# Seven products for eight in two gate and up blocks of each feed-forward stage

## The chip, the cores and the metric

The kernel runs on one core of a Trainium2 chip. The metric is the device time of one execution in microseconds, the median of three runs. A TensorE matmul here takes a 128x128 left operand and 512 columns of the right one, in float32r.

## The reference, cut to what matters

Two blocks over 256 tokens of width 1024 follow each other. Each is: feed-forward, mixer, feed-forward. The four feed-forward stages have this form, with `D_FF` = 2816:

```
def swiglu(x, w_gate, w_up, w_down):
    return (jax.nn.silu(x @ w_gate) * (x @ w_up)) @ w_down
x = x + 0.5 * swiglu(rms_norm(x, ffn1_norm[l]), ffn1_w_gate[l], ffn1_w_up[l], ffn1_w_down[l])
```

The first mixer is an attention with an indexer that picks 64 keys a query, beside a pool over windows; the second is a gated mixer with a short convolution. A final norm closes the program.

## The kernel before

Every product is done in three matmuls (`mm3`, L68): both operands are split into a high part that fits float32r and the rest, and hi*hi, hi*lo and lo*hi are summed in PSUM. Weights come in chunks of 128 x 2048 (1 MB). `weights` (L54) loads one from SP into a `raw` buffer (3 of them); `split` (L64) has ScalarE copy it into `whi` and VectorE subtract to `wlo` (4 pairs). The activations lie transposed and split in `hT`, written once a stage.

`rows` (L95) multiplies four k tiles of one chunk with both token tiles: 2 x 4 x 3 = 24 matmuls. In `ffn` (L219) blocks j = 0 to 4 hold 512 columns of gate and 512 of up, two chunks each for the two halves of the contraction; block 5 holds the last 256 of both in two chunks. `gated` (L226) applies Silu on ScalarE and the product on VectorE, both from PSUM; `turned` (L106) transposes the result on TensorE and splits it into `act`. Then the down projection runs in two halves f of six chunks. Work put in `late` (the transposes) is traced behind a later chunk by `flush` (L88). All PSUM tiles come from one rotation of eight banks, `ps` (L51).

Stage 1 starts with `cold_start` (L185), in pieces as the inputs land. The row norm is applied behind the matmuls: `rstd` (L133) takes a power on GpSimd (L86), and GpSimd does little else. The tables of the mixers are loaded from SP in the stage before (`meanwhile`, L260), the gain of the final norm in the last stage. At the end `y` (L722) is a `raw` buffer for each of the two token tiles; the four stores are issued at L736.

The program is written in a framework that takes the text as priority, works out the order on each engine and queue ahead of time by readiness, and sets the semaphores.

Of the kernel before, what the change touches and what calls it, by code (L numbers as in the profile page):

```python
# [10 lines left out]
F32 = mybir.dt.float32  # L11
# [6 lines left out]
P = 128  # L18
T = 256
# [15 lines left out]


class Block:
    def __init__(self, ctx, tc, a, out):
        self.tc, self.nc, self.a, self.out = tc, tc.nc, a, out
        pool = lambda name, bufs, **k: ctx.enter_context(tc.tile_pool(name=name, bufs=bufs, **k))  # L40
        self.const = pool("const", 1)
        self.raw = pool("raw", 3)
        self.wsp = pool("wsp", 4)
        self.big = pool("big", 1)
        self.work = pool("work", 2)
        self.small = pool("small", 4)
        self.psum = pool("psum", 8, space=PSUM)
        self.late = []


    def ps(self, shape=(P, 512)):  # L51
        return self.psum.tile(list(shape), F32, tag="ps", name="ps")

    def weights(self, src):  # L54

        n = src.shape[1]
        raw = self.raw.tile([P, 2048], F32, tag="raw", name="raw")[:, :n]
# [30 lines left out]
    def flush(self):  # L88

        late, self.late = self.late, []  # L90
        for f in late:
            f()
# [12 lines left out]

    def turned(self, dst, x, k):  # L106

        for t in range(2):
            n = x[t].shape[1] // P
            pt = self.ps((P, 4, P))  # L110
# [41 lines left out]
    def add(self, accs, f, scale, following, tiles=(0, 1)):  # L152
# [15 lines left out]
        def pair(k):  # L168
            pt = self.ps((P, 2, T))
# [6 lines left out]
        self.late += [lambda: pair(4 * f), lambda: pair(4 * f + 2)]  # L176


    def warm_up(self):

        ps = self.ps()
# [3 lines left out]
    def cold_start(self, accs, src):  # L185
# [33 lines left out]
    def ffn(self, n, following, first=False, meanwhile=None):  # L219
        nc, a = self.nc, self.a  # L220
        gu, d, d_end = a[f"gu{n}"], a[f"d{n}"], a[f"de{n}"]
        with self.tc.tile_pool(name="act", bufs=1) as pool:
            act = pool.tile([P, KF, 2, T], F32R, tag="act", name="act")
            r = None

            def gated(j, gs, us):  # L226
                prs = []
                for t in range(2):
                    w = gs[t].shape[1]
                    sg = self.work.tile([P, 512], F32, tag="sg", name="sg")[:, :w]  # L230
                    nc.scalar.activation(sg, gs[t], AF.Silu, scale=r[:, t : t + 1])  # L231
                    pr = self.work.tile([P, 512], F32, tag="pr", name="pr", bufs=4)[:, :w]
                    nc.vector.scalar_tensor_tensor(pr, us[t], r[:, t : t + 1], sg, op0=ALU.mult, op1=ALU.mult)  # L233
                    prs.append(pr)
                self.late.append(lambda: self.turned(act, prs, 4 * j))

            for j in range(6):
                G = [self.ps() for _ in range(2)]
                U = [self.ps() for _ in range(2)] if j < 5 else None
                if j == 0 and first:  # L240
                    self.cold_start((G, U), gu)
                    r = self.rstd()
                    gated(j, G, U)
                    continue
                self.token_major(G, gu[2 * j], 512, 0)
                self.flush()
                if j == 0:
                    self.token_major(U, gu[1], 512, 0)
                    self.flush()
                self.token_major(G, gu[2 * j], 512, 1)  # L250
                if j == 0:
                    r = self.rstd()
                elif j < 5:
                    self.token_major(U, gu[2 * j + 1], 512, 0)
                if j < 5:
                    self.token_major(U, gu[2 * j + 1], 512, 1)
                    gated(j, G, U)
                else:
                    gated(j, [x[:, :T] for x in G], [x[:, T:] for x in G])
                if j == 2 and meanwhile:  # L260
                    meanwhile()
            down = lambda f, c: self.weights(d[f, c] if c < 5 else d_end[f])
            for f in range(2):
                accs = [self.ps() for _ in range(2)]
                split = f == 1 and following == "final_norm_2"
                for c in range(4 if split else 6):
                    self.rows(accs, down(f, c), act, 4 * c, 4 if c < 5 else 2, KF - 1)
                    if c == 0:
                        self.flush()
                if split:  # L270
                    ws = [down(f, c) for c in (4, 5)]
                    for t in range(2):
                        for c in (4, 5):
                            self.rows(accs, ws[c - 4], act, 4 * c, 4 if c < 5 else 2, KF - 1, tiles=[t])
                        self.add(accs, f, 0.5, following, [t])
                else:
                    self.add(accs, f, 0.5, following)
# [12 lines left out]
    def mixer1_tables(self):  # L290
        nc, a, c1 = self.nc, self.a, self.c1
        load = lambda name, shape: self.load(c1, name, shape)
        cosq, sinq = load("cosq", [P, 2, 64]), load("sinq", [P, 2, 64])
        self.cosi, self.sini = load("cosi", [P, 2, 32]), load("sini", [P, 2, 32])
# [538 lines left out]
```

## Time and profile before

| what | value |
|---|---|
| median of three runs | 1094.07 us (1093.84 to 1094.1) |
| profiled execution | 1094.42 us |
| its span | 1092.6 us |
| mean granted clock of TensorE | 0.998 |
| busy: TensorE, VectorE, ScalarE, GpSimd | 99%, 56%, 46%, 1% of the span |
| read from DRAM | 199.88 MB |

A listing writes PE for TensorE, DVE for VectorE, ACT for ScalarE, POOL for GpSimd, SPq for SP's queue; PEld is a weight load. `out<-in` names tiles; an L number is a line of the kernel. Times count from the start of the span.

### The profile page before, as it was taken

To read this page: it belongs to the slowest core of one execution; us is meant where nothing else is said; L and a number is where in the kernel's file an instruction comes from. 1 tells how busy PE (TensorE), PEld (TensorE's weight loads), DVE (VectorE), ACT (ScalarE), POOL (GpSimd) and SP (SyncE) were. 2 spreads that over 40 slices of the span, in tenths; PEclk is the share of its full clock that TensorE was granted. 3 is DMA by queue.
4 is the path that set the end of the run, shared out by engine and by line. 5 is a ranking of instruction groups with operands and counts; after the bars stand their busy time and mean duration, and the time that the engine had idled before them with its cause. 6 is when DMAs were issued, how large, how long until landed. Compare 5 with 4: busy or idle time off the path is not lost.

```text
span 1092.6 us, 12852 instructions
## 1 busy us (share of the span) xinstructions
PE 1083.9 (99%) x5278; PEld 909.9 (83%) x5278; DVE 609.7 (56%) x660; ACT 507.6 (46%) x597; POOL 14.1 (1%) x28
## 2 busy tenths in 40 slices
PE   9999999999999999999999999999999999999997
PEld 8888888878888888888888888999888888888886
DVE  5755534796654554554554445777555465545552
ACT  7544433777454443444444344633454344444441
POOL 0000000010000000000000000000000000000000
PEclk9999999999999999999999999999999999999999
DMA  9765454634355555465555455454555545555441
GB/s 348 270 261 180 167 193 145 232 112 159 130 184 187 193 187 179 173 233 191 193 191 181 154 206 193 154 200 175 175 184 193 193 174 178 189 193 175 170 156 38
DMA packets 33178, 201.76 MB, mean 185 GB/s; under 512 B 4704, under 2 KB 5088, under 8 KB 10592
## 3 DMA queue, kind: packets, MB, share of 16 engines
q1 hardware_dynamic: 32688, 200.39, 51.8%
q8 instruction: 41, 0.67, 0.2%
q10 hardware_dynamic: 432, 0.55, 0.2%
q14 instruction: 17, 0.14, 0.0%
HBM read 199.88 MB, written 1.05 MB: 184 GB/s over the span
## 4 chain that ended last, share of the span: by engine, by line
PE 96%; DVE 1%; ACT 1%; issue 1%; DMA 0%; POOLq 0%; POOL 0%; ACTq 0%
PE ps L71 30%; PE ps L73 30%; PE ps L72 30%; PE ps L112 2%; PE ps L79 2%; PE ps L172 1%; DMA raw<-in_gu 0%; ACT ro L397 0%; DVE left L373 0%; DVE wlo L66 0%; PE ps L514 0%; ACT whi L65 0%; DVE m L371 0%; ACT rel L360 0%; ACT sqh L389 0%
## 5 line engine op out<-in xcount | busy, mean ns | idle before, releaser
L66 DVE TENSOR_TENSOR wlo<-raw,whi 128x2048 fp32r<-128x2048 f32 (+2 forms) x202 | 426.1, 2114 | 381.9 <-ACT whi L65 381.8
L65 ACT ACTIVATE whi<-raw 128x2048 fp32r<-128x2048 f32 (+2 forms) x202 | 357.1, 1772 | 421.4 <-PE ps L73 307.8
L71 PE MATMUL ps<-whi,hT 128*128 128x512 f32 (+1 forms) x912 | 357.0, 392 | 0.1
L72 PE MATMUL ps<-wlo,hT 128*128 128x512 f32 (+1 forms) x912 | 353.8, 388 | 0.2 <-DVE wlo L66 0.2
L73 PE MATMUL ps<-whi,hT 128*128 128x512 f32 (+1 forms) x912 | 353.9, 388 | 0.0
L71 PEld LDWEIGHTS ps<-whi,hT 128*128 128x128 f32 x912 | 171.4, 188 | 35.0 <-ACT sqh L389 0.3
L73 PEld LDWEIGHTS ps<-whi,hT 128*128 128x128 f32 x912 | 171.2, 188 | 35.2
L72 PEld LDWEIGHTS ps<-wlo,hT 128*128 128x128 f32 x912 | 171.4, 188 | 34.4 <-DVE wlo L66 0.5
L71 PE MATMUL ps<-whi,act 128*128 128x512 f32 x352 | 138.6, 394 | 0.0
L73 PE MATMUL ps<-whi,act 128*128 128x512 f32 x352 | 138.1, 392 | 0.0
L72 PE MATMUL ps<-wlo,act 128*128 128x512 f32 x352 | 138.0, 392 | 0.0
L73 PEld LDWEIGHTS ps<-whi,act 128*128 128x128 f32 x352 | 66.1, 188 | 14.7
L72 PEld LDWEIGHTS ps<-wlo,act 128*128 128x128 f32 x352 | 66.2, 188 | 14.6
L71 PEld LDWEIGHTS ps<-whi,act 128*128 128x128 f32 x352 | 66.1, 188 | 14.5
L231 ACT ACTIVATE sg<-ps,rstd 128x512 f32<-128x512 f32 (+1 forms) x48 | 31.3, 654 | 61.8 <-PE ps L73 45.8
L71 PE MATMUL ps<-hT,whi 128*128 128x256 f32 x192 | 54.4, 283 | 0.0
L72 PE MATMUL ps<-hT,whi 128*128 128x256 f32 x192 | 54.3, 283 | 0.0
L73 PE MATMUL ps<-hT,wlo 128*128 128x256 f32 x192 | 54.3, 283 | 0.0
L158 DVE SCALAR_TENSOR_TENSOR X<-ps,X 128x512 f32<-128x512 f32 x28 | 19.2, 688 | 42.4 <-PE ps L73 42.4
L233 DVE SCALAR_TENSOR_TENSOR pr<-ps,rstd,sg 128x512 f32<-128x512 f32 (+1 forms) x48 | 33.5, 703 | 12.1 <-PE ps L73 7.9
L72 PEld LDWEIGHTS ps<-hT,whi 128*128 128x128 f32 x192 | 36.9, 192 | 0.0
L71 PEld LDWEIGHTS ps<-hT,whi 128*128 128x128 f32 x192 | 36.9, 192 | 0.0
(155 smaller groups left out, 706.4 us busy)
## 6 DMA issues: line engine op xcount, KB each, us to landing
raw<-in_gu SPq DMA_DIRECT2D x84, 1024.0 KB, 4.8
raw<-in_d SPq DMA_DIRECT2D x40, 1024.0 KB, 4.7
raw<-in_w_out SPq DMA_DIRECT2D x8, 1024.0 KB, 5.0
raw<-in_w_cx SPq DMA_DIRECT2D x8, 1024.0 KB, 5.0
raw<-in_w_v SPq DMA_DIRECT2D x6, 1024.0 KB, 4.9
raw<-in_w_u SPq DMA_DIRECT2D x6, 1024.0 KB, 4.9
raw<-in_de SPq DMA_DIRECT2D x8, 512.0 KB, 3.5
raw<-in_w_b SPq DMA_DIRECT2D x4, 1024.0 KB, 4.9
```

Of the source, the lines that this page charges most:

```text
L65: self.nc.scalar.activation(hi, x, AF.Copy)
L66: self.nc.vector.tensor_tensor(lo, x, hi.bitcast(F32), op=ALU.subtract)
L71: mm(ps, lhsT=a[0], rhs=b[0], start=start, stop=False)
L72: mm(ps, lhsT=a[0], rhs=b[1], start=False, stop=False)
L73: mm(ps, lhsT=a[1], rhs=b[0], start=False, stop=stop)
L79: self.nc.tensor.matmul(ps, lhsT=a, rhs=b, start=start, stop=stop)
L112: self.nc.tensor.transpose(pt[:, i, :], x[t][:, i * P : i * P + P], self.ident)
L158: nc.vector.scalar_tensor_tensor(x, accs[t], scale, x, op0=ALU.mult, op1=ALU.add)
L172: nc.tensor.transpose(pt[:, i, t * P : t * P + P], self.X[t][:, (k + i) * P : (k + i) * P + P], self.ident)
L231: nc.scalar.activation(sg, gs[t], AF.Silu, scale=r[:, t : t + 1])
L233: nc.vector.scalar_tensor_tensor(pr, us[t], r[:, t : t + 1], sg, op0=ALU.mult, op1=ALU.mult)
```

## The change

Blocks 1 and 3 of each stage are computed as a product of 2 x 2 blocks: two token tiles by two halves of the contraction, times two halves of the contraction by gate and up. `quad` does it in seven products of 12 matmuls (four k tiles, one token tile, 512 columns) instead of eight. It needs sums on both sides. `combined` forms four combinations of the activations once a stage and splits them into `xc`. Of the weights, four quarters w11, w12, w21, w22 are loaded by GpSimd into a pool of four `blocks`; two of the sums are made by GpSimd transfers that add while they land (`accum_op`), w12 + b22 before product 2 and w11 + b12 after product 1 has split w11; two more are made in place on VectorE, before products 6 and 7. Each product's weights are split by themselves: seven splits a block instead of four. Results are copied out of PSUM and combined on VectorE.

The steps of a stage follow `ORDER`: a and b are steps of the quads of blocks 1 and 3, e, 2 and 4 plain chunks of blocks 5, 2 and 4, d chunks of the down projection, whose half f = 0 takes chunk 3 last. `flush` counts steps now, so transposes fall some steps later.

Around it: `raw` has two buffers instead of three, whi and wlo three instead of four; in the mixers `weights` takes every second buffer from a pool of two `blocks`. PSUM is divided into five banks `acc` and three `tmp`. The cold start loads into `blocks`. The mixers' tables are loaded in the mixers, behind their `rstd`, most of them from GpSimd; `fg` is a `raw` buffer at the end.

```
+ORDER = "eaeaa2a2aa2a244bb4bb4bdbdbdddddddddd"
...
-        self.raw = pool("raw", 3)
-        self.wsp = pool("wsp", 4)
+        self.raw = pool("raw", 2)
+        self.wsp = pool("wsp", 3)
         self.big = pool("big", 1)
         self.work = pool("work", 2)
         self.small = pool("small", 4)
-        self.psum = pool("psum", 8, space=PSUM)
+        self.psum = pool("psum", 1, space=PSUM)
...
+    def bank(self, tag, shape=(P, 512)):
+        return self.psum.tile(list(shape), F32, tag=tag, name=tag, bufs={"acc": 5, "tmp": 3}[tag])
+
     def ps(self, shape=(P, 512)):
-        return self.psum.tile(list(shape), F32, tag="ps", name="ps")
+        self.banks += 1
+        return self.bank("acc" if self.banks % 8 < 5 else "tmp", shape)
...
+        self.turn = not self.turn and self.spare
+        raw = self.block() if self.turn else self.raw.tile([P, 2048], F32, tag="raw", name="raw")
+        raw = raw[:, : src.shape[1]]
         self.nc.sync.dma_start(raw, src)
-        hi = self.wsp.tile([P, 2048], F32R, tag="whi", name="whi")[:, :n]
-        lo = self.wsp.tile([P, 2048], F32R, tag="wlo", name="wlo")[:, :n]
+        return self.parts(raw)
...
+    def parts(self, raw):
+        hi = self.wsp.tile([P, 2048], F32R, tag="whi", name="whi")[:, : raw.shape[1]]
+        lo = self.wsp.tile([P, 2048], F32R, tag="wlo", name="wlo")[:, : raw.shape[1]]
...
+    def flush(self, passed=99):
 
         late, self.late = self.late, []
-        for f in late:
-            f()
+        for n, f in late:
+            if n > passed:
+                self.late.append((n - passed, f))
+            else:
+                f()
+
+    def later(self, f, n=1):
+        self.late.append((n, f))
...
+    def combined(self, dst, x):
+        tt = self.nc.vector.tensor_tensor
+        whole = self.block().rearrange("p (k t) -> p k t", t=T)
+        tt(whole, x[:, :, 0, :].bitcast(F32), x[:, :, 1, :].bitcast(F32), op=ALU.add)
+        (x11, x21), (x12, x22) = [[whole[:, 4 * c : 4 * c + 4, t * P : t * P + P] for t in range(2)] for c in range(2)]
+        s = self.block().rearrange("p (k t) -> p k t", t=P)
+        s1, s2, s3, s4 = [s[:, 4 * i : 4 * i + 4, :] for i in range(4)]
+        tt(s1, x21, x22, op=ALU.subtract)
+        tt(s2, x11, s1, op=ALU.subtract)
+        tt(s3, x21, x11, op=ALU.subtract)
+        tt(s4, x12, s2, op=ALU.subtract)
+        yield
+        self.split(dst[:, :, 0, :], dst[:, :, 1, :], s)
+    def block(self, src=None):
+        b = self.blocks.tile([P, 2048], F32, tag="block", name="block")
+        if src is not None:
+            self.nc.gpsimd.dma_start(b, src)
+        return b
+    def quad(self, pool, b, x, xc):
+        nc, tt = self.nc, self.nc.vector.tensor_tensor
+        of_x = lambda c, t: lambda k: self.both(x[:, 4 * c + k, :, t * P : t * P + P])
+        of_xc = lambda i: lambda k: self.both(xc[:, 4 * i + k, :, :])
+        def product(left, w):
+            ps = self.bank("tmp")
+            for k in range(4):
+                c = slice(k * 512, k * 512 + 512)
+                self.mm3(ps, left(k), (w[0][:, c], w[1][:, c]), k == 0, k == 3)
+            return ps
+        p = lambda tag: pool.tile([P, 512], F32, tag=tag, name=tag)
+        def copy(ps, tag):
+            y = p(tag)
+            nc.scalar.activation(y, ps, AF.Copy)
+            return y
+        more = lambda w, src: nc.gpsimd.dma_start(w, src, accum_op=ALU.add)
+        (b11, b12), (b21, b22) = b
+        w11, w12, w22, w21 = self.block(b11), self.block(b12), self.block(b22), self.block(b21)
+        more(w12, b22)
+        y11 = copy(product(of_x(0, 0), self.parts(w11)), "p1")
+        more(w11, b12)
+        yield
+        p7 = copy(product(of_xc(2), self.parts(w12)), "p7")
+        yield
+        y12 = copy(product(of_xc(3), self.parts(w22)), "p3")
+        yield
+        y21 = p("p2")
+        tt(y21, product(of_x(1, 0), self.parts(w21)), y11, op=ALU.add)
+        y11, v = y21, y11
+        yield
+        p5 = copy(product(of_xc(0), self.parts(w11)), "p5")
+        yield
+        tt(w11, w11, w22, op=ALU.add)
+        tt(v, product(of_xc(1), self.parts(w11)), v, op=ALU.subtract)
+        yield
+        tt(w11, w11, w21, op=ALU.add)
+        w = self.parts(w11)
+        ps = product(of_x(1, 1), w)
+        tt(p7, p7, v, op=ALU.add)
+        tt(v, v, p5, op=ALU.add)
+        tt(p5, p7, p5, op=ALU.add)
+        tt(p7, ps, p7, op=ALU.subtract)
+        return y11, p7, y12, v, p5
...
-                raw = self.raw.tile([P, 2048], F32, tag="raw", name="raw")
+                raw = self.block()
...
+        with self.stage(4), self.tc.tile_pool(name="act", bufs=1) as pool:
             act = pool.tile([P, KF, 2, T], F32R, tag="act", name="act")
+            xc = pool.tile([P, 16, 2, P], F32R, tag="xc", name="xc")
...
+            def seven(j):
+                y11, y21, y12, x, y22 = yield from self.quad(pool, [[gu[2 * j + i, c] for i in range(2)] for c in range(2)], self.hT, xc)
+
+                def rest():
+                    tt = nc.vector.tensor_tensor
+                    tt(y12, y12, x, op=ALU.add)
+                    gated(j, silu([y11, y21]), [y12, y22])
+
+                self.later(rest, 3)
...
+                    order = (0, 1, 2, 4, 5, 3) if f == 0 else range(4 if split else 6)
+                    for c in order:
+                        if f or c:
+                            yield
+                        rows(c, w(c), 15 if f == 0 else KF - 1)
...
+            combined = self.combined(xc, self.hT)
+            next(combined)
+
+            steps = {"a": seven(1), "b": seven(3), "2": eight(2), "4": eight(4), "e": eight(5), "d": down()}
+            for step in ORDER:
+                next(steps[step], None)
+                self.flush(1 if step in "ab" else 2)
+                next(combined, None)
...
-        self.causal, self.ncausal = load("causal", [P, 2, T]), load("ncausal", [P, 2, T])
-        self.band, self.pw, self.pscale = load("band", [P, 4, 384]), load("pool_w", [P, 4, P]), load("pool_scale", [P, 4])
+        self.causal, self.ncausal = load("causal", [P, 2, T], nc.gpsimd), load("ncausal", [P, 2, T], nc.gpsimd)
+        self.band, self.pw = load("band", [P, 4, 384], nc.gpsimd), load("pool_w", [P, 4, P], nc.gpsimd)
+        self.pscale = load("pool_scale", [P, 4], nc.gpsimd)
...
+        load = lambda name, shape: self.load(self.c2, name, shape, self.nc.gpsimd)
...
+        fg = self.raw.tile([P, 2048], F32, tag="raw", name="fg")[:, :D]
+        nc.sync.dma_start(fg, a["final"].to_broadcast([P, D]))
```

## Rows read from the trace of the kernel before

**Rows 1.** The page: span, busy time of each engine, chain that ended last
```profile
span 1092.6 us, 12852 instructions
...
PE 1083.9 (99%) x5278; PEld 909.9 (83%) x5278; DVE 609.7 (56%) x660; ACT 507.6 (46%) x597; POOL 14.1 (1%) x28
...
PE 96%; DVE 1%; ACT 1%; issue 1%; DMA 0%; POOLq 0%; POOL 0%; ACTq 0%
```

**Rows 2.** Waits of TensorE's matmuls: us in total, times, longest
```profile
PE ps L72 <- DVE wlo L66: 0.2, 1, 0.2
```

**Rows 3.** Waits of VectorE and ScalarE in the weights' split
```profile
DVE wlo L66 <- ACT whi L65: 381.8, 148, 5.2
ACT whi L65 <- PE ps L73: 307.8, 95, 7.2
```

**Rows 4.** Busy us by stretch, with granted clock, DMA share, GB/s
```profile
core 0: us, PE busy (x) PEld busy (x) DVE busy (x) ACT busy (x) POOL busy (x), PEclk, DMA share, GB/s
10.00:20.00 10.00, 10.00 (x46) 8.29 (x45) 7.18 (x16) 9.03 (x21) 0.00 (x0) 1.00 1.05 395
...
317.00:425.00 108.00, 108.00 (x500) 89.86 (x499) 56.29 (x40) 47.27 (x40) 0.00 (x0) 1.00 0.52 181
...
215.00:250.00 35.00, 34.32 (x179) 27.87 (x176) 33.22 (x100) 26.76 (x87) 5.20 (x4) 1.00 0.43 158
```

**Rows 5.** Timeline of TensorE, first and last of 37 matmuls: start, us
```profile
311.29 0.39 PE L73 MATMUL ps<-whi,hT 128*128 128x512 f32 x1
...
319.44 0.39 PE L73 MATMUL ps<-whi,hT 128*128 128x512 f32 x1
```

**Rows 6.** Groups of VectorE by form: count, busy us, mean ns, idle before
```profile
L66 DVE TENSOR_TENSOR wlo<-raw,whi 128x2048 fp32r<-128x2048 f32 x176 | 403.1, 2291 | 359.3 <-ACT whi L65 359.1
...
L158 DVE SCALAR_TENSOR_TENSOR X<-ps,X 128x512 f32<-128x512 f32 x28 | 19.2, 688 | 42.4 <-PE ps L73 42.4
...
L673 DVE TENSOR_TENSOR m<-m 128x512 f32<-128x512 f32 x4 | 2.8, 692 | 0.1
```

**Rows 7.** Groups of ScalarE by form
```profile
L65 ACT ACTIVATE whi<-raw 128x2048 fp32r<-128x2048 f32 x176 | 336.9, 1915 | 392.4 <-PE ps L73 279.5 <-issue 80.3 <-PE ps L72 28.2
...
L65 ACT ACTIVATE act<-ps 128x512 fp32r<-128x512 f32 x40 | 21.4, 586 | 4.0 <-PE ps L112 4.0
```

**Rows 8.** Timeline, two splits in a row on VectorE and on ScalarE
```profile
30.26 4.48 DVE L66 TENSOR_TENSOR wlo<-raw,whi 128x2048 fp32r<-128x2048 f32 x2
...
24.69 3.71 ACT L65 ACTIVATE whi<-raw 128x2048 fp32r<-128x2048 f32 x2
```

**Rows 9.** Transfers: GB/s in 40 slices of 317 to 345 us; times to landing
```profile
GB/s 176 398 398 398 82 0 94 105 351 433 456 59 0 0 152 129 433 410 374 0 0 0 0 0 187 117 433 468 293 0 23 140 152 433 398 375 0 0 0 176
...
raw<-in_gu SPq DMA_DIRECT2D x5, 1024.0 KB, 4.8
...
DMA to landing us min/median/max: 2.0/2.2/2.5
```

**Rows 10.** Timeline of SP's queue, 0 to 60 us
```profile
15.42 13.86 SPq L58 DMA_DIRECT2D raw<-in_gu  x4
29.33 0.42 SPq L691 DMA_DIRECT2D cosq<-in_cosq  x1
32.57 11.25 SPq L58 DMA_DIRECT2D raw<-in_gu  x4
```

**Rows 11.** Timeline of GpSimd
```profile
298.62 0.69 POOL L86 TENSOR_TENSOR rstd<-var,mhalf 128x2 f32<-128x2 f32 x1 [61.34 <-DVE var L85]
```

**Rows 12.** Timeline of the last 9 us
```profile
1084.90 4.42 SPq L736 DMA_DIRECT2D out<-y  x3
...
1086.65 0.69 DVE L729 TENSOR_TENSOR y<-X,fg 128x512 f32<-128x512 f32 x1
...
1088.46 0.49 DVE L733 TENSOR_SCALAR y<-y,r 128x512 f32<-128x512 f32 x1 [0.66 <-POOL r L86]
1089.22 0.35 ACTq L736 DMA_DIRECT2D out<-y  x1
```

More of the change, by code (lines that the diff above doesn't have):

```diff
@@ L174, in pair @@
                 self.feed(k + i, pt[:, i, :], following)
-        self.late += [lambda: pair(4 * f), lambda: pair(4 * f + 2)]
+        for k in (4 * f, 4 * f + 2):
+            self.later(lambda k=k: pair(k), 3)
     def warm_up(self):
-        ps = self.ps()
+        ps = self.bank("tmp")
         for _ in range(WARM):
@@ L224, in ffn, with silu, gated @@
             r = None
-            def gated(j, gs, us):
+            def silu(gs):
+                sgs = []
+                for t in range(2):
+                    sg = self.work.tile([P, 512], F32, tag="sg", name="sg")[:, : gs[t].shape[1]]
+                    nc.scalar.activation(sg, gs[t], AF.Silu, scale=r[:, t : t + 1])
+                    sgs.append(sg)
+                return sgs
+            def gated(j, sgs, us):
                 prs = []
                 for t in range(2):
[L229 to L233, printed above, removed]
-                    prs.append(pr)
-                self.late.append(lambda: self.turned(act, prs, 4 * j))
@@ L262, in ffn @@
[L262 to L277, printed above, removed]
+                    pr = self.work.tile([P, 512], F32, tag="pr", name="pr", bufs=4)[:, : us[t].shape[1]]
@@ new lines, in gated, with eight @@
+                    nc.vector.scalar_tensor_tensor(pr, us[t], r[:, t : t + 1], sgs[t], op0=ALU.mult, op1=ALU.mult)
+                    prs.append(pr)
+                self.later(lambda: self.turned(act, prs, 4 * j), 2)
+            two = lambda: [self.bank("acc") for _ in range(2)]
+            def eight(j):
+                G = two()
+                self.token_major(G, gu[2 * j], 512, 0)
+                yield
+                self.token_major(G, gu[2 * j], 512, 1)
+                sgs = silu([x[:, :T] for x in G] if j == 5 else G)
+                if j < 5:
+                    yield
+                    U = two()
+                    self.token_major(U, gu[2 * j + 1], 512, 0)
+                    yield
+                    self.token_major(U, gu[2 * j + 1], 512, 1)
+                gated(j, sgs, [x[:, T:] for x in G] if j == 5 else U)
@@ new lines, in seven, with down @@
+            def seven(j):
[5 more added lines that the diff above has]
+                self.later(rest, 3)
+            def down():
+                for f in range(2):
+                    accs = two()
+                    w = lambda c: self.weights(d[f, c] if c < 5 else d_end[f])
+                    rows = lambda c, w, last, **k: self.rows(accs, w, act, 4 * c, 4 if c < 5 else 2, last, **k)
+                    split = f == 1 and following == "final_norm_2"
+                    order = (0, 1, 2, 4, 5, 3) if f == 0 else range(4 if split else 6)
+                    for c in order:
+                        if f or c:
+                            yield
+                        rows(c, w(c), 15 if f == 0 else KF - 1)
+                    if split:
+                        ws = [w(4), w(5)]
+                        for t in range(2):
+                            for c in (4, 5):
+                                rows(c, ws[c - 4], KF - 1, tiles=[t])
+                            self.add(accs, f, 0.5, following, [t])
+                    else:
+                        self.add(accs, f, 0.5, following)
@@ new lines, in ffn @@
+            G, U = two(), two()
+            if first:
+                self.cold_start((G, U), gu)
+            else:
+                self.token_major(G, gu[0], 512, 0)
+                self.flush()
+                self.token_major(U, gu[1], 512, 0)
+                self.flush()
+                self.token_major(G, gu[0], 512, 1)
+            r = self.rstd()
+            if not first:
+                self.token_major(U, gu[1], 512, 1)
+            gated(0, silu(G), U)
+            combined = self.combined(xc, self.hT)
```

85 lines of the change are left out of this document (30 added, 55 removed).

## The prediction

> **What bounds the kernel now.** I read the page first, for its shares and its chain. TensorE is busy 99% of the span and 96% of the chain that ended last is matmuls [rows 1]. The waits of TensorE say the same from the other side: the matmuls on a low weight half waited once, for 0.2 us [rows 2]. So time comes out only where matmuls are removed, or is lost where TensorE is made to wait. The waits of the other engines show what hides the weights' splitting: ScalarE's copy into whi sits idle 307.8 us for a matmul to give its buffer back, and VectorE waits 381.8 us for that copy [rows 3]. Both run as far ahead of TensorE as the buffers let them. The busy times by stretch show how much room they have: in 317 to 425 us, gate and up blocks only, VectorE works 56.29 of 108 us, ScalarE 47.27, and the DMA engines are busy for 0.52 of it [rows 4].
>
> **What a matmul costs.** The duration in the listing (0.39 us) is not the price, since matmuls overlap. The timeline gives starts: 36 matmuls lie between 311.29 and 319.44 us, 0.2264 us each [rows 5]. A plain chunk has 24 (two token tiles, four k, three matmuls of the split): 5.43 us. A product has 12: 2.72 us.
>
> The Trainium skill, page "TensorE: Matmul & The Clock Gate", section "Back-to-back issue gap", gives N/2.4 + 2.5 ns, which is 0.216 us for 512 columns; by it the 96 matmuls below would be worth 20.7 us. The row is 5% slower than the page, and the sum goes by the row.
>
> **What is removed.** A block of gate and up is eight products of 12 matmuls; a quad does seven. Two quads a stage, four stages: 8 x 12 = 96 matmuls, 96 x 0.2264 = 21.7 us. Nothing is added to TensorE: the transposes stay 8 a block, and the left operand (hT or xc) has the same 128x128 form.
>
> **What is added to VectorE and ScalarE.** A split of a chunk costs VectorE 2.29 us and ScalarE 1.92 us alone [rows 6, 7], and 2.24 and 1.86 in a run of two [rows 8]. Block by block: four splits become seven (3 x 2.29 = 6.9), two sums in place have the split's form (4.6), seven operations of 512 columns are at 0.69 (rows of such a sum in SBUF and of one that reads PSUM) (4.8) [rows 6]. That is 16.3 us more VectorE per quad. ScalarE has three splits and four 512-column copies at 0.59 more [rows 7], 8.1 us. Once a stage come the combined activations: a sum and a low half of 2048 columns, four of 512, 7.3 us on VectorE and 1.9 on ScalarE.
> By stage: 22 chunks at 56.29/19.9 = 2.83 us were 62 us of VectorE in 119.5 us of TensorE [rows 4]. Now 14 chunks (39.6), 14 splits (32.1), 4 sums (9.2), 14 small ones (9.7) and 7.3 make 98 us in 14 x 5.43 + 14 x 2.72 = 114 us: 86%. ScalarE has 14 x 2.38 + 14 x 1.9 + 8 x 0.59 + 1.9 = 66 us. On average both are covered by the matmuls, and cost nothing; the cover is gone where products stand side by side.
>
> **Where the cover is thin.** With three whi/wlo pairs a step's split can start when the step three before it has ended. Product 6 needs w11 + w22, which can only be formed once product 5 has split w11; product 7 needs a third value in the same tile. Each is a chain sum, copy, subtract: 2.3 + 1.9 + 2.3 = 6.5 us. The order of the first quad ends "a4 2 a5 a6 2 a7 2". Count from the end of a4. The step "2" runs to 5.4, a5 to 8.15. VectorE ends the low half of a5 at 1.4, y21 at 2.1, the first sum at 4.3; ScalarE copies to 6.3; the low half of a6 is there at 8.55, wanted at 8.4: 0.2 us late. Then the next "2" takes VectorE to 10.8, the second sum to 13.0, v to 13.7, and, since its copy is already there while that for a7 is not, the low half of the last "2" to 15.95, so that of a7 to 18.2. TensorE has done a6 and "2" at 16.5 and wants it at 16.75: 1.45 us late. So 1.7 us for the first quad. In the second, "b5 d b6 d b7", a plain chunk (5.4) and a product (2.7) run during each chain of 6.5: nothing late. Four stages: 7 us. The lower end is 0, should the scheduler have put the second sum ahead. The upper end is each chain started only when the step in front of its product starts: 3.8 + 1.1 us in a first quad, 2 x 1.1 in a second, 28 us in all. I take 7: the row of one stretch shows splits running a buffer ahead [rows 3], not starting late.
>
> **The GpSimd transfers.** Before has none. The nearest row is a 1 MB load from SP, landing in 4.8 us, at some 400 GB/s while it moves [rows 9], so 2.6 us of the engines. Four quarters and two accumulating ones a quad replace four loads: 4 MB more a stage. A plain quarter should cost as much as the row; an accumulating one also reads its target, so between the row (4.8) and anything; I take twice. The cover: w12 and its addition are wanted at product 2, three plain chunks and a product after the stage's first ScalarE work, over 20 us after the blocks are free; the addition into w11 between products 1 and 5, some 19 us. In the gate and up stretch 14 + 8 plain loads take 22 x 2.6 = 57 of 114 us; the four accumulations have 57 us, 14 each. Price of the transfers: 0.
> Queues. Each engine's order is set by readiness and not by the program text: the table cosq, written behind block 2, went out at 29.33 us between weight loads [rows 10]. So quarters for the second quad go out as soon as blocks are free. Queued with them on GpSimd is the power in rstd, which waited 61.34 us idle before [rows 11]; an issue that waits for a split would hold it, and behind it Silu and the gate's two PSUM banks. The early issues (w11, w12) wait for nothing of the new stage, and w22 waits for the combined sum, later than the power. I take 0, at worst the landing time, 4.8 us a stage. The tables that leave SP, and the mixers' memsets behind them on GpSimd, have whole chunks of cover.
>
> **Fewer buffers elsewhere.** raw 3 to 2 and whi/wlo 4 to 3. In a run of plain chunks a load goes out when the split two chunks before it is done, and lands 4.9 us later; the splits still start when a buffer is given back, so no loss. Thin is the first mixer: in 215 to 250 us VectorE works 33.22 of 35 us [rows 4], and one chunk less ahead may cost from 0 to that chunk, 5.4 us; the waits there were near 0 [rows 2], so I take 1.
> The tail: fg and both y now share two raw slots, so y of the second tile waits for the first tile's stores. They went out from 1084.90 and land after 2.1 to 2.5 [rows 9, 12], by 1087.6; its two multiplications (0.69) then end at 1088.95, where the last scaling began at 1088.46 [rows 12]: 0.4 us, from 0 to 2.
>
> **The sum.** The profiled execution took 1094.42 us, 1.8 us around a span of 1092.6 [rows 1]; the median of the runs is 1094.07. 1094.4 - 21.7 + 7.0 + 1.0 + 0.4 = 1081.1, against the median some 1081.
>
> **The rivals.**
> All hidden. The order puts the sums early enough, and only the tail remains: 1094.1 - 21.7 + 0.4 = 1073. For it speaks that 14% of VectorE's time is free in the stretch; against it the chain of a7.
> VectorE binds in the quads. It is 86% busy over the stretch, and each late low half pushes what stands behind it in its fixed order, evictions too, so TensorE waits in second quads as well. From the upper end, 28 us: 1101; with half of it 1087. It turns the change into a loss from 2.7 us a quad.
> The accumulating transfers bind, the case on the other side. Place: the addition into w12 before product 2, and into w11 before product 5. It decides from 14 us each, where the DMA engines have no time left; at 20 us each the stretch gets 57 + 80 - 114 = 23 us longer in every stage, 92 us in all, less the 21.7: about 1164; at 16 us each 1100. For it: no row shows one, and 10 to 20 us in the cold start shows the engines at a share of 1.05 with 395 GB/s [rows 4], so there is a ceiling. Against: three times the row's transfer time would still fit.
> The page "DMA: Bandwidth & Descriptors" of the Trainium skill, section "Issuing engines are not separate DMA queues", says that transfers issued by GpSimd run on the same 16 engines as SP's. By that rule the second queue adds no bandwidth, as this rival has it; no run here shows GpSimd's queue beside SP's.
> The change does do what it says: 96 matmuls fewer are in the text of the loops.
>
> **How the numbers follow.** Forecast (3 to 14 us given back) 0.55, own range 1075 to 1087. All hidden 0.17. VectorE binds 0.18: a third of that still ahead by over 0.2% (2.2 us, about what a measurement here can tell from no change), 0.04 within it, 0.08 behind. Transfers bind 0.10. Faster 0.55 + 0.17 + 0.06 = 0.78, same 0.04, slower 0.08 + 0.10 = 0.18. Low end 1072, the whole saving with nothing given back; high end 1094, where the cases left out (slower) hold 0.18.
>
> **What the new profile would show.** 5182 matmul records in place of 5278, with 0.2264 us between starts inside a product. Waits of TensorE for wlo at the sixth and seventh product of each first quad, under 2 us; if they stand in second quads too, the second rival. Low halves still 2.29 us; VectorE near 86% in the gate and up stretches. If whi or the sum in place waits for a DMA of w11 or w12, the third. The prediction is wrong if TensorE waits at stage borders, where I priced nothing.

## The result and the profile after

The changed kernel took 1135.03, 1135.82 and 1140.91 us (a fourth run, at 1336.67 with a granted clock of 0.751, was disturbed and is left out) against 1094.09 before: a ratio of 1.0395, 95% interval 1.0358 to 1.0431. It is slower by 4%, some 43 us, where 1081 us was forecast. Times below are medians; a difference between two kernels is that of their ratios to the kernel before, times 1094.1.

The page of the changed kernel, for [rows 1]; below busy times and clock the chain:
```profile
span 1133.3 us, 12907 instructions
...
PE 1081.6 (95%) x5182; PEld 900.8 (79%) x5182; DVE 758.3 (67%) x780; ACT 576.0 (51%) x657; POOL 51.2 (5%) x85
...
PEclk9999999999998999999989999999999999999999
...
PE 70%; DVE 10%; DMA 10%; issue 5%; ACT 4%; POOL 0%; SPq 0%; POOLq 0%; ACTq 0%; DVEq 0%
```
The 96 matmuls are gone, yet TensorE is busy almost as long over a longer span, since some matmuls now run at half the clock (its mean granted clock is 0.983, before 0.998). A tenth of the chain is DMA, where before it was 0% [rows 1]. TensorE's waits, us in total, times and longest, against the single 0.2 us of [rows 2]:
```profile
PE tmp L210 <- DVE pr L338: 26.6, 10, 4.1
PE tmp L83 <- ACT whi L77: 4.3, 4, 1.1
PE acc L85 <- DVE hT L223: 3.2, 1, 3.2
PE acc L84 <- DVE wlo L78: 1.9, 3, 1.1
PE tmp L84 <- DVE wlo L78: 1.6, 4, 0.4
PE acc L83 <- ACT mT L77: 1.6, 1, 1.6
PE acc L85 <- DVE mT L78: 1.2, 1, 1.2
```
Most of the waiting is not for a weight half. It stands in front of the transposes (L210), for the product of gate and up (pr), the last step before them on VectorE.

**The first long gap.** The second feed-forward stage, GpSimd's timeline, for [rows 11]:
```profile
312.37 0.70 POOL L98 TENSOR_TENSOR rstd<-var,mhalf 128x2 f32<-128x2 f32 x1 [61.70 <-DVE var L97]
313.32 1.13 POOL L151 DMA_DIRECT2D block<-in_gu  x2 [0.25 <-issue]
326.45 0.53 POOL L151 DMA_DIRECT2D block<-in_gu  x1 [12.00 <-DVE block L144]
330.86 0.53 POOL L151 DMA_DIRECT2D block<-in_gu  x1 [3.87 <-DVE xc L78]
331.37 0.93 POOL L175 DMA_DIRECT2D block<-in_gu  x1
```
w11 and w12 are issued at 313.32. The addition into w12 (L175) needs nothing but w12, but GpSimd issues in order, and before it stand w22 and w21, whose blocks hold the combined activations: 12.00 us of wait for one, 3.87 for the other. So it goes out at 331.37, some 17 us behind w12's load. ScalarE's timeline:
```profile
343.25 1.92 ACT L77 ACTIVATE whi<-block 128x2048 fp32r<-128x2048 f32 x1 [3.34 <-DMA block<-in_gu]
345.07 0.46 ACT L330 ACTIVATE sg<-acc,rstd 128x256 f32<-128x256 f32 x1
```
The split of w12 waits for the addition to land, 11.8 us after its issue, with Silu behind it; on VectorE pr stands behind the low half:
```profile
345.20 2.29 DVE L78 TENSOR_TENSOR wlo<-block,whi 128x2048 fp32r<-128x2048 f32 x1 [7.14 <-ACT whi L77]
347.41 0.87 DVE L338 SCALAR_TENSOR_TENSOR pr<-acc,rstd,sg 128x256 f32<-128x256 f32 x2
```
So pr of a block whose last matmul began at 344.33 comes at 347.41, because both engines do their work in a fixed order. TensorE:
```profile
344.33 0.39 PE L85 MATMUL acc<-whi,hT 128*128 128x512 f32 x1
347.95 1.12 PE L210 MATMUL tmp<-ident,pr 128*128 128x128 f32 x4 [3.23 <-DVE pr L338]
...
349.44 0.63 PE L84 MATMUL tmp<-wlo,xc 128*128 128x512 f32 x1
...
353.70 0.45 PE L85 MATMUL tmp<-whi,xc 128*128 128x512 f32 x1
```
3.4 us are lost in the gap, and behind it ten matmuls lie 0.43 us apart (349.44 to 353.70), not 0.2264: two more. The windows (busy us, granted clock, DMA share, GB/s):
```profile
331.00:345.00 14.00, 13.72 (x65) 11.13 (x63) 5.91 (x5) 4.67 (x5) 2.16 (x3) 1.00 0.94 243
...
350.00:354.00 4.00, 4.00 (x12) 3.09 (x11) 3.34 (x4) 0.05 (x1) 0.00 (x0) 0.52 0.53 223
...
375.00:395.00 20.00, 16.80 (x75) 13.38 (x74) 14.36 (x12) 7.45 (x4) 1.95 (x3) 0.99 0.84 282
...
1018.00:1022.00 4.00, 2.59 (x13) 1.82 (x11) 3.00 (x3) 3.87 (x5) 0.00 (x0) 1.00 0.55 231
```
While the additions move, the DMA engines are busy for 0.94 of the time at 243 GB/s; a stretch of plain loads had 395 GB/s at 1.05 [rows 4]. Behind the gap the clock is 0.52, the 1.2 GHz level. Not every gap is followed by that: behind one of as good a length in the last stage (3.4 us, ending at 1017.63) it stayed at 1.00, the last row.

**The second long gap**, 2.3 us at 391.25, has the same shape with another cause. ScalarE's splits behind the first quad's sums:
```profile
376.20 1.91 ACT L77 ACTIVATE whi<-block 128x2048 fp32r<-128x2048 f32 x1 [1.89 <-DVE block L195]
378.02 1.90 ACT L77 ACTIVATE whi<-raw 128x2048 fp32r<-128x2048 f32 x1
388.21 1.92 ACT L77 ACTIVATE whi<-raw 128x2048 fp32r<-128x2048 f32 x1 [8.29 <-DMA raw<-in_gu]
393.18 1.91 ACT L77 ACTIVATE whi<-raw 128x2048 fp32r<-128x2048 f32 x1 [3.06 <-DMA raw<-in_gu]
```
A raw load went out at 361.67 and the next only at 378.34: the chunk in the other raw buffer had its low half at 376.02, behind a sum of the quad (373.81) in VectorE's order, and only then was the buffer free. The load landed beside the transfers for the second quad, and VectorE once more had the late low half ahead of pr, for which TensorE waited:
```profile
390.16 2.29 DVE L78 TENSOR_TENSOR wlo<-raw,whi 128x2048 fp32r<-128x2048 f32 x1 [4.32 <-ACT whi L77]
...
392.97 0.74 DVE L338 SCALAR_TENSOR_TENSOR pr<-acc,rstd,sg 128x512 f32<-128x512 f32 x1
...
393.77 0.66 PE L210 MATMUL tmp<-ident,pr 128*128 128x128 f32 x4 [2.13 <-DVE pr L338]
```

Stage by stage, from the last transposes of X ahead of each stage, in profiled executions (the last four rows are runs told below):

| us | ffn1 | mixer1 | ffn2 | ffn3 | mixer2 | ffn4, end |
|---|---|---|---|---|---|---|
| before | 198.3 | 100.8 | 186.4 | 187.9 | 232.4 | 186.9 |
| after | 206.4 | 106.4 | 193.6 | 195.4 | 235.4 | 196.1 |
| no quads, blocks kept | 196.5 | 105.9 | 187.3 | 188.1 | 235.0 | 189.1 |
| VectorE's sums, new order | 197.3 | 106.6 | 185.9 | 187.0 | 235.8 | 187.5 |
| addition first, new order | 202.4 | 105.4 | 183.0 | 183.9 | 237.2 | 186.6 |
| best | 198.0 | 101.0 | 183.4 | 183.8 | 232.1 | 185.1 |

### The profile page after: what moved, and what is told of

The parts are those of the page before. It is cut to its first block, busy times and chain, and to the rows that moved or that the text cites. A ratio compares the mean times of both kernels' runs of the same rounds, so it can differ in the third digit from the quotient of the medians.

```text
span 1133.3 us, 12907 instructions
## 1 busy us (share of the span) xinstructions
PE 1081.6 (95%) x5182; PEld 900.8 (79%) x5182; DVE 758.3 (67%) x780; ACT 576.0 (51%) x657; POOL 51.2 (5%) x85
## 3 DMA queue, kind: packets, MB, share of 16 engines
HBM read 216.66 MB, written 1.05 MB: 192 GB/s over the span
## 4 chain that ended last, share of the span: by engine, by line
PE 70%; DVE 10%; DMA 10%; issue 5%; ACT 4%; POOL 0%; SPq 0%; POOLq 0%; ACTq 0%; DVEq 0%
PE acc L85 16%; PE acc L83 16%; PE acc L84 16%; PE tmp L83 6%; PE tmp L84 6%; PE tmp L85 6%; DVE wlo L78 6%; DMA block<-in_gu 5%; DMA raw<-in_gu 4%; ACT whi L77 3%; PE tmp L210 2%; PE acc L91 1%; DMA raw<-in_d 1%; DVE xc L78 1%; DVE block L192 1%
## 5 line engine op out<-in xcount | busy, mean ns | idle before, releaser
L78 DVE TENSOR_TENSOR wlo<-raw,whi 128x2048 fp32r<-128x2048 f32 (+1 forms) x127 | 282.2, 2222 | 175.4 <-ACT whi L77 175.4
L77 ACT ACTIVATE whi<-raw 128x2048 fp32r<-128x2048 f32 (+1 forms) x127 | 236.3, 1860 | 244.3 <-PE acc L85 106.8
L78 DVE TENSOR_TENSOR wlo<-block,whi 128x2048 fp32r<-128x2048 f32 (+2 forms) x99 | 198.5, 2013 | 100.4 <-ACT whi L77 100.3
L85 PE MATMUL acc<-whi,hT 128*128 128x512 f32 (+1 forms) x608 | 238.1, 392 | 3.2 <-DVE hT L223 3.2
L83 PE MATMUL acc<-whi,hT 128*128 128x512 f32 (+1 forms) x608 | 240.0, 396 | 0.5 <-ACT whi L77 0.4
L84 PE MATMUL acc<-wlo,hT 128*128 128x512 f32 (+1 forms) x608 | 238.4, 392 | 1.3 <-DVE wlo L78 1.3
L77 ACT ACTIVATE whi<-block 128x2048 fp32r<-128x2048 f32 (+2 forms) x99 | 166.7, 1691 | 107.5 <-PE acc L85 27.3
L84 PE MATMUL acc<-wlo,act 128*128 128x512 f32 x352 | 137.1, 389 | 0.6 <-DVE wlo L78 0.6
L83 PE MATMUL acc<-whi,act 128*128 128x512 f32 x352 | 137.6, 391 | 0.0
L85 PEld LDWEIGHTS acc<-whi,hT 128*128 128x128 f32 x608 | 115.8, 190 | 27.0 <-DVE hT L223 3.6
L85 PE MATMUL acc<-whi,act 128*128 128x512 f32 x352 | 136.9, 392 | 0.1
L83 PEld LDWEIGHTS acc<-whi,hT 128*128 128x128 f32 x608 | 116.2, 191 | 24.3 <-ACT hT L222 0.8
L85 PEld LDWEIGHTS acc<-whi,act 128*128 128x128 f32 x352 | 66.1, 188 | 15.2 <-DVE act L78 1.6
L83 PEld LDWEIGHTS acc<-whi,act 128*128 128x128 f32 x352 | 66.1, 188 | 13.3
L210 PE MATMUL tmp<-ident,pr 128*128 128x128 f32 x176 | 27.9, 296 | 26.6 <-DVE pr L338 26.6
```

The lines of the kernel that those rows point to most:

```text
L77: self.nc.scalar.activation(hi, x, AF.Copy)
L78: self.nc.vector.tensor_tensor(lo, x, hi.bitcast(F32), op=ALU.subtract)
L83: mm(ps, lhsT=a[0], rhs=b[0], start=start, stop=False)
L84: mm(ps, lhsT=a[0], rhs=b[1], start=False, stop=False)
L85: mm(ps, lhsT=a[1], rhs=b[0], start=False, stop=stop)
L210: self.nc.tensor.transpose(pt[:, i, :], x[t][:, i * P : i * P + P], self.ident)
```

## The experiments

The theory: the additions go out late, and the fixed orders of ScalarE and VectorE turn that into late Silus and a late pr; raw loads go out late around the quads' sums; the clock halves behind long gaps; and the mixers lose by late tables and fewer buffers. The rivals: VectorE binds in the quads; the accumulating transfers cost the same wherever they stand.

**The addition first.**
```
-        w11, w12, w22, w21 = self.block(b11), self.block(b12), self.block(b22), self.block(b21)
+        w11, w12 = self.block(b11), self.block(b12)
         more(w12, b22)
+        w22, w21 = self.block(b22), self.block(b21)
```


> The addition into w12 is written ahead of the loads of w22 and w21, so GpSimd issues it one place earlier in its order (in the first stage, two). Theory (the additions are late because they stand in GpSimd's order behind loads that wait, and ScalarE's fixed order then holds Silu; late raw loads beside the transfers; half the clock behind each long gap): the addition goes out some 4 us earlier, the wait of whi for block and the gap of TensorE of 3.4 us in front of the first transposes of each stage go, with the slow clock behind it; the other gap, at the raw loads, stays: 1114 to 1122 us. Rival (VectorE binds in the quads): no change, 1130 or more. Rival (an addition costs its time wherever it is put, since the DMA engines are full): the same time within 5 us, with the gap in another place.


1127.09 us, ratio 1.0296: 11 us less. The gap of 3.4 us in the second stage shrank to 0.8. Less than the 14 to 22 that were expected: from the second stage on the addition still stands behind w22, the second gap stayed, and in the first stage, where the addition now waited for w12's own load, TensorE's longest wait grew from 4.1 to 4.7 us.

**Additions as plain transfers.** `more` without `accum_op`, so that the two sums are left out and their bytes still move.


> Leaves out the adding of the two transferred weight sums: the same transfers, in the same places, overwrite their targets in place of adding. Isolates what the accumulating costs over a plain transfer of the same bytes. Theory: landing falls from 10.6 us to 5 to 6 us, the wait of whi for block before the second product shrinks below 1 us and the raw loads beside the transfers land in 5 us: 1100 to 1115 us. Rival (VectorE binds): the same 1136 within 3 us. Rival (the fewer buffers and the moved tables cost it): the same 1136.


1113.03 us, ratio 1.0181: 23 us less with all instructions in the same order, so this is what the accumulating costs over plain transfers there. The second gap stayed (TensorE idle 2.1 us at 385): it has another cause. The transfers of L175, in the changed kernel and then in this one:
```profile
L175 POOL DMA_DIRECT2D block<-in_gu x16: 858/877/932, 31.6 to 1027.2; - x16
...
  ACT whi L77: 11.7, 4
...
DMA to landing us min/median/max: 7.7/10.6/17.6
```
```profile
L175 POOL DMA_DIRECT2D block<-in_gu x16: 530/530/530, 32.2 to 1005.7; - x16
...
  ACT whi L77: 1.1, 1
...
DMA to landing us min/median/max: 5.0/6.0/13.7
```

**Sums on VectorE.**
```
-        more(w12, b22)
...
-        more(w11, b12)
+        tt(w11, w11, w12, op=ALU.add)
+        tt(w12, w12, w22, op=ALU.add)
```


> The two weight sums that GpSimd's transfers made are formed in place by VectorE (two more operations of 2048 columns a quad, 4.6 us); the four quarters stay GpSimd's plain loads, so DMA traffic is that of the kernel before. Theory (transfers): gaps in front of the second product and at the raw loads go; VectorE goes from 67% to some 70% and adds late sums of its own, 2 to 4 us a first quad: 1100 to 1118 us. Rival (VectorE binds): slower than 1136, by up to 8 x 4.6 = 37 us.


1120.8 us, ratio 1.0249: 16 us less, with 16 operations of 2.29 us (37 us) added to the engine that the rival names as the bound. So VectorE's work is not what made the changed kernel slow. It isn't free either: this run is 7 us above the one with plain transfers. The time is just above the range of the theory.

**No quads.** Blocks 1 and 3 plain, in a row.
```
+ORDER = "eeaaaa22224444bbbbdddddddddddd"
-            steps = {"a": seven(1), "b": seven(3), ...
+            steps = {"a": eight(1), "b": eight(3), ...
```


> Blocks 1 and 3 are plain blocks again, in a row, with no combined activations and no GpSimd quarters or sums; the fewer buffers, the split of the PSUM banks, the moved tables and the first chunks' blocks stay. Gives the price of what stands around the quads. Theory: the two mixers hold some 10 us of the loss and the tail 0.4, the feed-forward stages nothing: 1101 to 1108 us. Rival (the fewer buffers and banks hurt in the feed-forward stages too): 1115 or more.


1116.55 us, between the two. One gap of 7.2 us, at the second mixer's start, was the experiment's own: with no blocks allocated, act lies where the mixer's first loads go. So it was run again with one column of each of the four blocks written by GpSimd:


> The kernel without quads (1116.6 us) once more, with its four blocks a stage kept allocated (GpSimd writes one column of each), so that the next stage's first loads do not wait for the memory of act, which in that kernel cost a gap of 7.2 us at the second mixer's start. Gives the price of what stands around the quads. Theory (mixers and start of the first stage): 1103 to 1109 us. Rival (fewer buffers in the feed-forward stages): 1114 or more.


1106.25 us, ratio 1.0106. TensorE's waits in it:
```profile
PE acc L85 <- DVE hT L223: 3.0, 1, 3.0
PE acc L83 <- ACT mT L77: 1.6, 1, 1.6
PE acc L85 <- DVE mT L78: 1.2, 1, 1.2
```
What stands around the quads costs 12 us; of the 9.3 us in the profiled execution 7.7 are in the mixers (table). So the quads cost 0.0289 x 1094.1 = 32 us net, and with the 21.7 saved give back 53.

**A new order of the first quad**, on VectorE's sums.
```
-ORDER = "eaeaa2a2aa2a244bb4bb4bdbdbdddddddddd"
+ORDER = "eaea2aa2a2a2a44bb4bb4bdbdbdddddddddd"
```


> On the kernel with VectorE's sums (1120.8 us): the order of the first quad is changed from a2 a3 2 a4 2 a5 a6 2 a7 2 to a2 2 a3 a4 2 a5 2 a6 2 a7, so that a plain chunk and a product run during each chain of sum, copy and subtract, as in the second quad. Theory: the two gaps behind the sixth product (0.6 and 1.25 us a stage) go, the one at the raw loads stays or moves by a chunk: 1112 to 1117 us. Rival (VectorE is the bound of the stretch, the order only says where it shows): the same 1121 within 2 us.


1102.15 us, ratio 1.0076: 19 us less than with the old order, over twice what was expected, with the same work on every engine. What ScalarE waited for raw loads, in the changed kernel, with VectorE's sums, and with the new order (one row of each view):
```profile
ACT whi L77 <- DMA raw<-in_gu: 52.3, 10, 9.4
```
```profile
ACT whi L77 <- DMA raw<-in_gu: 25.9, 6, 6.1
```
```profile
ACT whi L77 <- DMA raw<-in_gu: 0.9, 1, 0.9
```
With a plain chunk between the sums the raw buffers come free in time, and the second gap is gone.

**Three raw buffers**, paid with a block (w21 in w12's place).
```
+        self.raw = pool("raw", 3)
         p7 = copy(product(of_xc(2), self.parts(w12)), "p7")
+        w21 = self.block(b21, "B")
```


> On the kernel with VectorE's sums (1120.8 us): raw gets its third buffer back; the memory comes from the quads, whose blocks go from four to three (w21 takes w12's place behind the second product). Theory (two raw buffers make the loads of the plain chunks behind the first quad late, ScalarE's copy waits 5.1 and 3.8 us for them, and Silu and pr behind it): the gaps of 1.5 to 2.9 us some 45 us into each stage go, with the slow clock behind them: 1104 to 1112 us. Rival (these gaps are VectorE's): 1118 or more.


1116.19 us, ratio 1.0211, 4 us less than without. The wait moved from the raw loads to the blocks:
```profile
ACT whi L77 <- DMA block<-in_gu: 23.7, 11, 3.6
...
ACT whi L77 <- DMA raw<-in_gu: 1.2, 3, 0.5
```
The second gap went as the theory has it, and one of 3.6 to 3.8 us came at the quad's start: with three blocks w11 takes the place of the combined sum and goes out at 319.28, 14 us behind rstd, and the sums of the weights come later with it.

**The mixers' buffers**, and then everything at once. Every fourth whi/wlo pair from the mixers' blocks; the tables' products by `nc.gpsimd`.


> On the changed kernel (1136 us): the two mixers get four whi/wlo pairs again (the fourth in place of the spare blocks) and the tables qC, qS, kC, kS are formed by GpSimd in place of VectorE, so that VectorE's low halves of hT do not stand behind the table's DMA. The feed-forward stages stay. Theory: the gap of 3.3 us at the first mixer's start and those of 2.4 and 1.4 at the second's end go, with the clock behind them: 1125 to 1130 us. Rival (the mixers lose by the GpSimd tables' traffic): 1133 or more.


1142.91 us, ratio 1.0442: 5 us more, with intervals that overlap, and no gain. Giving the blocks to the fourth pair left the mixers two raw buffers in place of four. The first gap of the second stage grew to 6.8 us: it is the late addition again, issued at 336.90 and split at 352.07, after 6.72 us of ScalarE's waiting. Which of the edits made it land later wasn't settled.


> VectorE's sums, the new order of the first quad, three raw buffers and three blocks, four pairs in the mixers and GpSimd's tables, all together. Theory (the parts add up: 16 us, some 5, some 12 and some 9 from 1136): 1086 to 1096 us, about the kernel before. Rival (VectorE binds in the quads once the transfers do not): 1105 or more.


1119.16 us, ratio 1.0226. It holds the gap of the three blocks, 3.3 to 3.8 us, in three stages, and in the first mixer 4.0 us at the transposes of R. The rival's number, but not its reason: VectorE has no more work here than at 1102.

**The accumulating transfers with the new order**, with the addition first and then without.


> The changed kernel with GpSimd's accumulating transfers kept, the addition into w12 written ahead of w22 and w21 (as in the run at 1127) and the new order of the first quad (as in the run at 1102). Theory (the order was most of what was left, and an early enough accumulating transfer is hidden): 1104 to 1114 us. Rival (the accumulating transfers fill the DMA engines wherever they stand, so that the order helps little): 1118 or more. Rival (VectorE's 4.6 us a quad are what the run at 1102 still pays): below 1100.


1100.19 us, ratio 1.0051: 38 us less than the changed kernel, below the range of the theory, and no slower than with VectorE's sums in that order (1102.15).


> The changed kernel (1136 us) with the new order of its first quad alone; the additions stay where they were. Theory (two separate losses: the late addition into w12, worth the 10 us that putting it first gave, and the order): the order's 18 to 27 us come off, the gap in front of the first transposes of 3.4 us stays: 1108 to 1118 us. Rival (with a plain chunk more ahead of the third product the late addition is covered too): 1097 to 1103, as with both.


1113.86 us, ratio 1.0175: the order alone brings 24 us, and the first gap stays, 2.6 to 2.9 us. So place and order are two losses, 11 and 24 us alone and 38 together. The raw loads show what the order does, against 52.3 us in the changed kernel:
```profile
ACT whi L77 <- DMA raw<-in_gu: 11.0, 5, 3.6
```

**The first mixer's tables loaded at the start**, with VectorE's sums and with the transfers.


> On the kernel with VectorE's sums and the new order (1102.15 us): the first mixer's cosq, sinq and norm rows are loaded at the kernel's start (room from junk, which takes sg's buffers), so that VectorE's tables wait for no transfer at the mixer's start. Theory: the gap of 3.4 us at the first mixer's low halves of hT goes, with the slow clock behind it: 1095 to 1099 us. Rival (fewer whi/wlo pairs make VectorE late there anyway): 1101 or more.

> The accumulating transfers, the earlier addition, the new order and the tables loaded at the start, together. Theory: 4 to 6 us below the same kernel with late tables, 1099 to 1109 us. Rival: the same as that kernel.


1104.84 (ratio 1.0096) and 1099.58 us (1.0051). The gap of 2.6 to 3.4 us went in both; a new one of 2.2 us came in the first stage's down product (act, at 161 us). No gain as a whole, as the rivals' numbers have it, but not for the first rival's reason: with as few buffers as ever the first mixer took 101.0 us in both, against 100.8 before, and the first stage took longer instead (with VectorE's sums 205.9 in place of 197.3, with the transfers 204.4 in place of 202.4).

**No quads in the first stage**, where they still lose (202.4 against 196.5 in the table); the second mixer's output c by c. Most of the loss there is the addition's: in the run at 1100.19 it waited for w12's own load, ScalarE then for it, and TensorE stood 2.8 and 1.9 us behind:
```profile
31.57 0.93 POOL L175 DMA_DIRECT2D block<-in_gu  x1 [5.92 <-DMA block<-in_gu]
...
44.28 1.92 ACT L77 ACTIVATE whi<-block 128x2048 fp32r<-128x2048 f32 x1 [5.78 <-DMA block<-in_gu]
```
With VectorE's sums in the same order that stage took 197.3. VectorE's sums there and transfers in the later stages were not tried together.
```
+            block = eight if first else seven
-        for f in range(2):
-            for c in range(2):
+        for c in range(2):
+            for f in range(2):
                 w = self.weights(a["w_out_2"][f, c])
```


> From the kernel at 1099.6 us: no quads in the first feed-forward stage (plain chunks, 24 matmuls more, 5.4 us), and the second mixer's output products run c by c, so that a chunk that needs nothing new stands behind the transposes of mT. Theory (from the starts of the two mixers in the run without quads and in that with the new order, quads lose 5.9 us net in the first stage and gain 4.1 in each later one; the second mixer's two gaps are 3.1 us): 1086 to 1092 us, faster than before by 0.3 to 0.7%. Rival (the plan of the other stages changes with it, and the gaps move): 1095 or more.

> The same with VectorE's sums in place of the accumulating transfers, which leaves no transfer more than in the kernel before. Theory: one gap more a stage (1.3 to 1.6 us where ScalarE's copy waits for VectorE's sum), 3 stages: 2 to 6 us above its twin, 1089 to 1096. Rival (accumulating transfers still cost more than VectorE's 4.6 us): below its twin.


1091.95 us (0.9983, 0.9974 to 0.9992) and 1099.14 us (1.0048). Once their places are right, the transfers beat VectorE's sums by 7 us. The two mixer gaps had stayed, since two of the four accumulators were tmp banks; the last run takes acc banks and puts a plain block's transposes one chunk later in the first stage:
```
-        accs = [[self.ps() for _ in range(2)] for _ in range(2)]
+        accs = [[self.bank("acc") for _ in range(2)] for _ in range(2)]
```


> The run at 1091.95 us with two edits outside the quads: the four accumulators of the second mixer's output come from the acc banks, so that TensorE's order puts a chunk that waits for nothing behind the transposes of mT, and in the first stage the transposes of a plain block stand one chunk later. Theory (the gaps of 1.7 and 1.4 us there and of 1.4 us in the first stage go, nothing else moves): 1086 to 1089 us, faster than before by 0.5 to 0.7%. Rival (the gaps only move): 1091 to 1093.


1085.61 us, ratio 0.9937 (0.9919 to 0.9954; one of six runs took 1092.09): 7 us faster than before, with 72 matmuls fewer (16.3 us). TensorE's waits in it:
```profile
PE acc L85 <- DVE wlo L79: 5.6, 7, 1.1
PE tmp L92 <- POOL mhalf L837: 1.0, 1, 1.0
```

## Why the prediction was wrong, point by point

**Right.** 5182 matmuls, and within a product at the full clock 0.2264 us between starts (362.16 to 363.97 for eight), as in [rows 5]. VectorE's pieces, for [rows 6]:
```profile
L78 DVE TENSOR_TENSOR wlo<-raw,whi 128x2048 fp32r<-128x2048 f32 x119 | 272.4, 2289 | 161.7 <-ACT whi L77 161.7
L78 DVE TENSOR_TENSOR wlo<-block,whi 128x2048 fp32r<-128x2048 f32 x81 | 185.4, 2288 | 94.9 <-ACT whi L77 94.9
...
L195 DVE TENSOR_TENSOR block<-block 128x2048 f32<-128x2048 f32 x8 | 18.3, 2288 | 0.1
```
VectorE rose by 148.6 us; the prediction's 36 a stage are 144. The chains of sums for the first quad's products 6 and 7 cost 0.56 + 1.24 = 1.8 us at 373 to 378 us, against 0.2 + 1.45. That the second number came near is in part luck: TensorE waited there not for a low half, as was counted, but for the high half of product 7, since its order has that product's first matmul two matmuls into the plain chunk before it:
```profile
378.17 0.51 PE L83 MATMUL tmp<-whi,hT 128*128 128x512 f32 x1 [1.07 <-ACT whi L77]
```
rstd was not held: from the second stage on GpSimd computed it before any quarter was issued, and in the first only a quarter's issue of 0.53 us came right before it.

**Failed: "Price of the transfers: 0".** The size was about right, twice the row having been taken: 10.6 us to landing against 4.8 [rows 9]. Wrong was the cover of "over 20 us after the blocks are free". The prediction itself had w22 waiting for the combined sum, and looked only at what that holds up in rstd, not at the addition behind it on the same queue. From its issue at 331.37 to the time ScalarE was free for it (343.25 - 3.34 = 339.91) the cover was 8.5 us. With the adding left out 23 us came back, with the addition moved by one place 11. `whi` waiting for w12's transfer is also the sign that the prediction gave for its third rival.

**Failed: "the splits still start when a buffer is given back, so no loss" for raw.** That holds in a run of plain chunks, where it was argued (187.3 us for the second stage without quads, 186.4 before). Beside a quad the split of a plain chunk stands in fixed orders behind a sum and behind splits that wait for one, so a raw buffer stays full and its next load goes out late. The chain of sums was priced at its own lateness of 1.7 us; what it does to raw loads, pr and transposes was not. The new order brought 24 us.

**Not priced: the clock.** The sum has no term for it. Of the eight gaps of over 2 us in the feed-forward stages six were followed by five to ten matmuls some 0.43 us apart, one by three (972.21) and one by none (1017.63). In the second stage four gaps lost 7.5 us, and 17 such steps some 3.5 more. Over the run the mean granted clock fell by 0.015, an estimate of 17 us at 1133 us, part of it inside the gaps, where it costs nothing.

**Failed: tables with "whole chunks of cover".** Around the quads 12 us are lost (the run without them), 5.1 in the first mixer and 2.6 in the second. In the first VectorE stood 4.5 us for qg's transfer, issued only at 205.19, at the stage's end, with the low halves of hT behind it. The 1.0 for fewer buffers was not the term that failed: with the tables early and the buffers as few, the first mixer took 101.0 us, 0.2 more than before. In the second mixer the division of PSUM mattered, for which the sum has no term: with two of the output's accumulators in tmp banks it took 235.7, with all four in acc banks 232.1 (both c by c), before 232.4. That TensorE waits at a stage border (3.2 us for hT) is the sign that the prediction itself named for being wrong.

**Mis-sized: the tail.** Priced at 0.4, it took 9.2 us from the last sum into X (1124.13) to the end, against 6.7 (1085.92): 2.5.

**The rivals.** The one on the other side named the place, the addition before product 2, but set its price from 14 us of landing each, as if the DMA engines had to be full over the stretch. 10.6 us were enough, because a fixed order makes lateness out of what is only badly placed. The page "DMA: Bandwidth & Descriptors" of the Trainium skill, section "Issuing engines are not separate DMA queues", has GpSimd's transfers on the same engines as SP's; the trace agrees, with a raw load that SP issued at 335.65 us landing after 11.7 us beside three transfers that GpSimd issued from 330.86 to 333.72, where the median of these loads is 4.9. "VectorE binds in the quads" fell, as the cause of the loss, with the two runs that gave VectorE more work and were 16 and 35 us faster than the changed kernel.

## What to carry to other kernels

An asynchronous step is covered from its issue, not from when its operands are free: list what stands before it on its queue, and what each of those waits for. Then follow one late item down the fixed order of the engine that consumes it: a weight split 3 us late held pr, the transposes and, through the clock, the matmuls behind them. And price a saving stage by stage: here 5.4 us a stage became a gain of about 4, against the run without quads, in the three later stages, and a loss in the first, which had the same order but its addition late.

## What had not been expected of the hardware

An accumulating transfer of 1 MB took 10.6 us to land and 877 ns of GpSimd to issue, a plain one in its place 6.0 us and 530 ns, and with accumulating ones about the DMA engines moved 243 GB/s at a share of 0.94. After a gap of 3.4 us the granted clock was 0.52 for some 4 us, after another as long it stayed at 1.00, in a program that had 1.00 in every stretch read before [rows 4].
